# Deferring the last plain column block's eviction into the first Strassen-like unit of each FFN, with its gate product on VectorE

## Chip, cores and metric

One core of one Trainium2 chip. The metric is the device time of one execution in microseconds (us), the median of several runs; lower is better.

## What is computed

Two transformer blocks on x (512 tokens, width 1024), in float32. Three gated feed-forward networks (FFN) stand in them: f0 closes the first block, f1 opens the second, f2 closes the second.

```
def swiglu(xn, w_gate, w_up, w_down):
    return (jax.nn.silu(xn @ w_gate) * (xn @ w_up)) @ w_down    # hidden width 2816 = 22 blocks of 128
```

Between and before them are attention, retention and gating mixers, which the change doesn't touch.

## The kernel before

**Numbers.** Every float32 operand of a product is split into a high part of reduced precision (ScalarE casts it) and a low part (the rest, by a subtraction on VectorE or GpSimd). A product is three matmuls: high by high, high by low, low by high.

**An FFN** (function `ffn`, L1324) runs over the 22 hidden column blocks in two halves of 11. Blocks 0 to 4 of the first half are *plain* (`NPLAIN = 5`): gate and up projections of 128 columns by 512 tokens, each 24 matmuls into one PSUM bank. Blocks 5 to 10 and the whole second half are *units* (function `unit`, L1239): gate and up of a block are computed together as a 2 by 2 block product with seven quarter products of 12 matmuls (128x256) in place of eight. In the order of issue they are B11, T1, T2, B21, B22, T3 and T4; T4 of a unit is issued in the middle of the next one. After each half come the down products.

**A plain block's eviction** (L1363 to L1370): VectorE multiplies the gate bank by the norm factors (`fg`, L1365), ScalarE takes tanh of half of it (`ft`, L1366), VectorE does the same multiplication for the up bank (`u`, L1367), GpSimd multiplies `u` by `fg` (L1368), VectorE forms `ft = (ft + 1) * u` (L1369), and `put_hidden` (L1316) writes the high part `hh` on ScalarE (L365) and the low part `hl` on VectorE (L372). `hh` and `hl` are read by the down products, much later. For block 4, `prepare_b` (L1220) stands ahead of the eviction: it splits the eight normed inputs into `xh` (ScalarE, L363) and `xl` (VectorE, L370), which the units read.

**A unit** (L1250 to L1294) puts B11 into bank `r1` and ScalarE copies it out (`fu`, L1251); T1 goes into the right half of bank `r23` and ScalarE copies it out (`ff`, L1256); T2 is added to `r1`, which is copied out (`fu`, L1267); B21 goes into the left half of `r23`, B22 onto its right half; VectorE then forms the gate (`fg`, L1279); T3 is added to `r1`, read by L1285. Between these the unit prepares the next unit's weights: ScalarE casts the raw weights `wh<-raw` (parts AB), then `wh<-s13f` (parts S13), later `wh<-s24f` (parts S24); the low parts of AB are two GpSimd subtractions, those of S13 and S24 one VectorE subtraction each (all L303). `parts_d` casts `whd` on ScalarE, with the low part `wld` on GpSimd, for this unit's own T4. The raw buffers so freed release the next loads on SyncE's queue (L194). There are four raw buffers and five buffers of parts.

After T1 a unit calls `self.flush()`, which runs what an earlier step left in `self.pending` (the T4 of the unit before), and runs what that returns (that unit's `put_hidden`) after T2's copy:

```
self.quarter(r23[:, 256:512], u.S13, 0, "T1", True)
nc.scalar.copy(f, r23[:, 256:512])
...
late = self.flush()
...
self.quarter(r1, u.S24, 0, "T2", False)
nc.scalar.copy(e[:, 256:512], r1)
if late is not None:
    late()
u.parts_d()
```

At the first unit of an FFN nothing is pending. What sets the order of work: engines run their queues in order. A compile-time scheduler orders instructions of no further constraint by their place in the program and their readiness by its own estimate; from the first unit of a run of units to the last, `in_order` (L1307) fixes each engine's instructions in the order in which they were traced. Block 4's eviction is traced ahead of that region. The PSUM dependence goes by bank: a matmul that writes one half of `r23` waits for a copy that reads the other half.

The place in question occurs three times per execution, once in each FFN: the step from plain block 4 to unit 5, below called an *entry*.

Of the kernel before, what the change touches and what calls it, by code (L numbers as in the profile page):

```python
# [13 lines left out]
ALU = mybir.AluOpType  # L14
# [16 lines left out]
NPLAIN = 5  # L31
# [302 lines left out]
class Build:  # L334
# [145 lines left out]
    def plan(self):  # L480
# [63 lines left out]
        for m in range(KD):  # L544
            feat(f"o{m}", "w_out", m * P)
        ffn("f0", "w_ffn_down")
        ffn("f1", "ffn1_w_down_2")
        tok("t20", "w_in_2", KD, 1408, 1536, (1664, 1840))
        for key, c in (("kc", 1024), ("vc", 1152), ("ks", 1280), ("kw", 1536)):
# [16 lines left out]
        for m in range(KD):  # L566
            feat(f"o2{m}", "w_out_2", m * P)
        ffn("f2", "ffn2_w_down_2", True)
        return out

# [753 lines left out]
    def ffn(self, tag, scale, gain, hooks, on_out, begun=None, each=None, last=None):  # L1324
        nc, att = self.nc, self.att
        n = 0
        self.th, self.tl, self.ynorm = [], [], {}
        for half in range(2):
            hh, hl = [], []
            for i in range(11):  # L1330
                if half or i >= NPLAIN:
                    if i in (0, NPLAIN):
                        start = len(self.traced())
                    self.unit(f"{tag}{half}{i}", hh, hl, i)
                    if i == 10:
                        self.in_order(start)
                        self.last_step = [x for x in self.traced() if x.engine == mybir.EngineType.DVE][-1]
                    continue
                acc = []
                for w in "gu":  # L1340
                    wh, wl = self.ws.next(f"{tag}{w}{half}{i}")
                    self.ws.run_ahead()
                    if i == 1:

                        if w == "g":
                            early = self.ps.tile([P, 1024], F32, tag="ss", name=self.nm("early"), bufs=2)
                        b = early[:, 512 * (w == "u"):512 * (w == "u") + 512]
                    else:
                        b = self.bank("mm")
                    self.drain(self.tgroup(b, [(wh[:, k, :], wl[:, k, :], self.xh[k], self.xl[k]) for k in range(KD)]))  # L1350
                    acc.append(b)
                    if n < len(hooks):
                        hooks[n]()
                    n += 1
                    if n == 2 * NPLAIN - 1:
                        u = self.first_unit(f"{tag}0{NPLAIN}")
                        u.hi24()
                        u.lo24()
                if i == 0 and begun is not None:
                    begun()  # L1360
                if i == NPLAIN - 1:
                    self.prepare_b()
                tl = lambda t, bufs=1: att.tile([P, 512], F32, tag=t, name=self.nm(t), bufs=bufs)  # L1363
                g, th, u = tl("fg"), tl("ft", 2), self.small.tile([P, 512], F32, tag="sq", name=self.nm("u"), bufs=1)
                nc.vector.tensor_tensor(out=g, in0=acc[0], in1=self.rb, op=ALU.mult)  # L1365
                nc.scalar.activation(th, g, AF.Tanh, scale=0.5)  # L1366
                nc.vector.tensor_tensor(out=u, in0=acc[1], in1=self.rb, op=ALU.mult)  # L1367
                nc.gpsimd.tensor_tensor(out=u, in0=u, in1=g, op=ALU.mult)  # L1368
                nc.vector.scalar_tensor_tensor(out=th, in0=th, scalar=1.0, in1=u, op0=ALU.add, op1=ALU.mult)  # L1369
                self.put_hidden(i, th, 0.5, hh, hl)  # L1370
                if i < 4:
                    self.prepare_t(i, gain)
            if half == 1 and last is not None:
                last(hh, hl)
                return
            for m in range(KD):
                b = self.bank("mm")
                for p, (k0, k1) in enumerate(((0, 6), (6, 11))):
                    wh, wl = self.ws.next(f"{tag}d{half}{m}")
                    self.ws.run_ahead()  # L1380
                    for k in range(k0, k1):
                        self.mm3(b, wh[:, k - k0, :], wl[:, k - k0, :], hh[k], hl[k], k == 0, k == 10)
                    if m == 0 and p == 0:
                        self.flush()()
                    if half == 0 and (m, p) == (KD - 2, 1):
                        u = self.first_unit(f"{tag}10")
                    if half == 0 and (m, p) == (KD - 1, 0):
                        u.hi24()
                        u.lo24()
                x = self.xs[m]  # L1390
                if half == 0 and each is not None:
                    with self.tc.issue_after(self.last_step):
                        each(half, m)
                if scale == 1.0:
                    nc.vector.tensor_tensor(out=x, in0=b, in1=x, op=ALU.add)
                else:
                    nc.vector.scalar_tensor_tensor(out=x, in0=b, scalar=scale, in1=x, op0=ALU.mult, op1=ALU.add)
                if half == 1:
                    on_out(m, x)
# [659 lines left out]
```

## Time and profile before

| what | value |
|---|---|
| median of 3 runs | 2061.87 us (2060.95 to 2062.26) |
| the profiled execution's own time | 2062.82 us |
| its span, first to last instruction | 2061.0 us |
| TensorE (PE) busy | 98% |
| VectorE (DVE) / ScalarE (ACT) / GpSimd (POOL) busy | 71% / 50% / 27% |
| mean granted TensorE clock | 0.996 of full speed |

Busy times are shares of the span. A PE matmul's end is modelled: consecutive matmuls overlap in the records, so starts are the better measure of its pace. The clock column is the share of full speed (2.4 GHz) that was granted; the lower level is 1.2 GHz, 0.5 of it.

### The profile page before, as it was taken

How to read it: one execution, taken by the hardware profiler on the slowest of the kernel's cores; microseconds unless marked ns; L12 is line 12 of the kernel's file. 1: busy time of each engine (PE TensorE's matmuls, PEld its weight loads, DVE VectorE, ACT ScalarE, POOL GpSimd, SP SyncE). 2: the span in 40 equal slices, each digit the busy share in tenths (PEclk: the TensorE clock that was granted, in tenths of full speed). 3: DMA queues.
4: the chain of work that ended last, by engine and by line, in shares of the span. 5: the costliest groups of instructions: out<-in, count | busy, mean ns of one | idle time of the engine just before them, and what ended most of it. 6: DMA issues, size and time to landing. Idle time of an engine off the chain costs nothing. (4 is left out here: it accounts for less than half of the span.)

```text
span 2061.0 us, 31305 instructions
## 1 busy us (share of the span) xinstructions
PE 2019.5 (98%) x11694; PEld 1746.3 (85%) x11694; DVE 1466.9 (71%) x2727; ACT 1040.6 (50%) x1944; POOL 550.1 (27%) x463
## 2 busy tenths in 40 slices
PE   9999999999999999999999999999999999999998
PEld 7787878889899889899987778888888888989997
DVE  7678776686487487668648799888557757756865
ACT  7666753354355435335435576666343333533554
POOL 1233233331132333124235211110312233312310
PEclk9999999999999999999999999999999999999999
DMA  6323254214234322333455313222543442232353
GB/s 202 77 69 96 90 162 132 90 60 117 92 103 122 114 72 90 105 99 102 129 160 157 96 54 86 77 67 72 171 131 103 125 146 72 85 111 94 106 176 127
DMA packets 229527, 223.60 MB, mean 108 GB/s; under 512 B 16784, under 2 KB 190992, under 8 KB 229376
## 3 DMA queue, kind: packets, MB, share of 16 engines
q1 hardware_dynamic: 222992, 203.94, 32.9%
q0 software_dynamic: 5024, 15.90, 2.4%
q10 hardware_dynamic: 1360, 1.77, 0.3%
q8 instruction: 92, 1.51, 0.3%
q14 instruction: 59, 0.48, 0.1%
HBM read 204.11 MB, written 14.68 MB: 106 GB/s over the span
## 5 line engine op out<-in xcount | busy, mean ns | idle before, releaser
L236 DVE TENSOR_TENSOR wl<-raw,wh 128x1024 fp32r<-128x1024 f32 (+5 forms) x267 | 321.4, 1206 | 164.8 <-ACT wh L235 163.7
L235 ACT CAST wh<-raw 128x1024 fp32r<-128x1024 f32 (+5 forms) x267 | 252.2, 948 | 359.5 <-PE mm L397 289.5
L396 PE MATMUL mm<-xh,wh 128*128 128x512 f32 x888 | 363.0, 409 | 1.8 <-ACT th L363 1.4
L397 PE MATMUL mm<-xl,wh 128*128 128x512 f32 x888 | 349.8, 394 | 1.9 <-DVE xl L370 1.9
L398 PE MATMUL mm<-xh,wl 128*128 128x512 f32 x888 | 350.2, 395 | 0.0
L303 POOL TENSOR_TENSOR wl<-raw,wh 128x512 fp32r<-128x512 f32 x102 | 133.4, 1329 | 267.1 <-PE mm L1195 152.0
L398 PEld LDWEIGHTS mm<-xh,wl 128*128 128x128 f32 x888 | 167.0, 188 | 35.5
L396 PEld LDWEIGHTS mm<-xh,wh 128*128 128x128 f32 x888 | 167.6, 189 | 29.8 <-ACT th L363 2.6
L397 PEld LDWEIGHTS mm<-xl,wh 128*128 128x128 f32 x888 | 167.8, 189 | 28.3 <-DVE xl L370 3.7
L397 PE MATMUL mm<-hl,wh 128*128 128x512 f32 x440 | 172.8, 393 | 0.8 <-DVE hl L372 0.8
L398 PE MATMUL mm<-hh,wl 128*128 128x512 f32 x440 | 172.9, 393 | 0.0
L396 PE MATMUL mm<-hh,wh 128*128 128x512 f32 x440 | 171.2, 389 | 0.0
L613 ACT ACTIVATE P<-s,st 128x128 f32<-128x128 f32 (+1 forms) x192 | 101.3, 529 | 58.3 <-DVE st L608 54.2
L303 POOL TENSOR_TENSOR wld<-raw,whd 128x512 fp32r<-128x512 f32 x51 | 69.5, 1362 | 217.6 <-ACT whd L300 130.3
L1195 PE MATMUL pt<-xh,wh 128*128 128x256 f32 x408 | 114.9, 282 | 7.2 <-ACT ff L1256 7.2
L1195 PE MATMUL pt<-xl,wh 128*128 128x256 f32 x408 | 114.8, 281 | 0.0
L1195 PE MATMUL pt<-xh,wl 128*128 128x256 f32 x408 | 114.8, 281 | 0.0
L1195 PE MATMUL mm<-th,wh 128*128 128x256 f32 x408 | 113.3, 278 | 0.0
L1195 PE MATMUL mm<-tl,wh 128*128 128x256 f32 x408 | 112.9, 277 | 0.0
L1195 PE MATMUL mm<-th,wl 128*128 128x256 f32 x408 | 112.8, 276 | 0.0
L363 ACT CAST ph<-pt 128x128 fp32r<-128x128 f32 x192 | 80.3, 424 | 55.0 <-PE pt L631 53.8
L451 POOL TENSOR_TENSOR sacc<-sacc,sq 128x512 f32<-128x512 f32 x36 | 57.2, 1589 | 165.5 <-ACT sq L449 162.8
(482 smaller groups left out, 5462.3 us busy)
## 6 DMA issues: line engine op xcount, KB each, us to landing
raw<-in_gu_f SPq DMA_DIRECT2D x132, 512.0 KB
raw<-in_w_in SPq DMA_DIRECT2D x79, 512.0 KB
raw<-in_ffn_w_down SPq DMA_DIRECT2D x22, 512.0 KB
raw<-in_ffn_w_down SPq DMA_DIRECT2D x24, 384.0 KB
sp_th<-gt SPq DMA_DIRECT2D x32, 256.0 KB
raw<-in_w_out SPq DMA_DIRECT2D x16, 512.0 KB
raw<-in_ffn_w_down SPq DMA_DIRECT2D x24, 320.0 KB
raw<-in_w_ffn_down SPq DMA_DIRECT2D x16, 384.0 KB
```

The costliest lines, as they stand in the source:

```text
L235: nc.scalar.copy(p[0][:, :nk * nc_], src)
L236: nc.vector.tensor_tensor(out=p[1][:, :nk * nc_], in0=src, in1=p[0][:, :nk * nc_].bitcast(F32), op=ALU.subtract)
L303: (eng or self.ws.b.nc.vector).tensor_tensor(out=p[1], in0=src, in1=p[0].bitcast(F32), op=ALU.subtract)
L363: self.nc.scalar.copy(out, in_)
L396: mm(acc, lhsT=lh, rhs=rh, start=start, stop=False)
L397: mm(acc, lhsT=lh, rhs=rl, start=False, stop=False)
L398: mm(acc, lhsT=ll, rhs=rh, start=False, stop=stop)
L451: (eng or nc.gpsimd).tensor_tensor(out=acc, in0=acc, in1=dst, op=ALU.add)
L613: nc.scalar.activation(p, b, AF.Exp, bias=st[:, 0:1], scale=-1.0, accum_out=st[:, 1:2])
L1195: self.nc.tensor.matmul(acc, lhsT=l[:, sl], rhs=r, start=start and k + n == 0, stop=k == 3 and n == 2, skip_group_check=True)
```

## The change

For block 4 alone, the last three steps of the eviction (the product of `u` and `fg`, the `ft` step, `put_hidden`) are no longer traced ahead of the first unit. They are put into `self.pending`, so that unit 5 runs the product and the `ft` step after T1 and its copy `ff`, and `put_hidden` after T2 and its copy `fu`. The product of block 4 goes from GpSimd to VectorE. Blocks 0 to 3 run as before.

```
--- before.py
+++ after.py
@@ -1365,9 +1365,16 @@
                 nc.vector.tensor_tensor(out=g, in0=acc[0], in1=self.rb, op=ALU.mult)
                 nc.scalar.activation(th, g, AF.Tanh, scale=0.5)
                 nc.vector.tensor_tensor(out=u, in0=acc[1], in1=self.rb, op=ALU.mult)
-                nc.gpsimd.tensor_tensor(out=u, in0=u, in1=g, op=ALU.mult)
-                nc.vector.scalar_tensor_tensor(out=th, in0=th, scalar=1.0, in1=u, op0=ALU.add, op1=ALU.mult)
-                self.put_hidden(i, th, 0.5, hh, hl)
+
+                def close(i=i, g=g, th=th, u=u):
+                    (nc.vector if i == NPLAIN - 1 else nc.gpsimd).tensor_tensor(out=u, in0=u, in1=g, op=ALU.mult)
+                    nc.vector.scalar_tensor_tensor(out=th, in0=th, scalar=1.0, in1=u, op0=ALU.add, op1=ALU.mult)
+                    return lambda: self.put_hidden(i, th, 0.5, hh, hl)
+
+                if i == NPLAIN - 1:
+                    self.pending = close
+                else:
+                    close()()
                 if i < 4:
                     self.prepare_t(i, gain)
             if half == 1 and last is not None:
```

## Rows read from the trace of the kernel before

**Rows 1.** The page: busy time of each engine, its share and instructions.

```profile
PE 2019.5 (98%) x11694; PEld 1746.3 (85%) x11694; DVE 1466.9 (71%) x2727; ACT 1040.6 (50%) x1944; POOL 550.1 (27%) x463
```

**Rows 2.** Waits of PE, by line waited for: us in total, times, longest.

```profile
PE pt L1195 <- ACT ff L1256: 7.2, 3, 2.4
PE mm L396 <- DVE feat L852: 3.4, 2, 2.7
PE s L1618 <- DVE blkhl L370: 2.4, 1, 2.4
```

**Rows 3.** Timeline of PE, third entry: start us, us, ..., [idle before <- releaser].

```profile
1763.32 0.28 PE L1195 MATMUL pt<-th,wl 128*128 128x256 f32 x1
...
1764.88 0.28 PE L1195 MATMUL mm<-th,wl 128*128 128x256 f32 x1
...
1767.57 0.44 PE L1195 MATMUL pt<-xh,wh 128*128 128x256 f32 x1 [2.40 <-ACT ff L1256]
```

**Rows 4.** Timeline of ACT, third entry.

```profile
1766.62 0.63 ACT L365 ACTIVATE hh<-ft 128x512 fp32r<-128x512 f32 x1 [3.20 <-DVE ft L1369]
1767.16 0.35 ACT L1256 COPY ff<-pt 128x256 f32<-128x256 f32 x1
1767.41 1.05 ACT L300 CAST wh<-raw 128x1024 fp32r<-128x1024 f32 x1
...
1769.27 0.38 ACT L1267 COPY fu<-mm 128x256 f32<-128x256 f32 x1
1769.53 0.64 ACT L300 CAST whd<-raw 128x512 fp32r<-128x512 f32 x1
1770.25 1.01 ACT L300 CAST wh<-s24f 128x1024 fp32r<-128x1024 f32 x1
```

**Rows 5.** Timeline of DVE, third entry.

```profile
1763.44 0.68 DVE L1367 TENSOR_TENSOR u<-mm,rb 128x512 f32<-128x512 f32 x1
1764.05 0.68 DVE L370 TENSOR_TENSOR xl<-y,xh 128x512 fp32r<-128x512 f32 x1
1765.90 0.69 DVE L1369 SCALAR_TENSOR_TENSOR ft<-ft,u 128x512 f32<-128x512 f32 x1 [1.17 <-POOL u L1368]
...
1769.41 1.23 DVE L303 TENSOR_TENSOR wl<-s13f,wh 128x1024 fp32r<-128x1024 f32 x1 [1.43 <-ACT wh L300]
...
1775.42 0.69 DVE L284 TENSOR_TENSOR s13f<-raw 128x512 f32<-128x512 f32 x1
```

**Rows 6.** Timeline of POOL, third entry.

```profile
1764.27 1.59 POOL L1368 TENSOR_TENSOR u<-u,fg 128x512 f32<-128x512 f32 x1 [8.15 <-DVE u L1367]
1768.54 2.54 POOL L303 TENSOR_TENSOR wl<-raw,wh 128x512 fp32r<-128x512 f32 x2 [2.67 <-ACT wh L300]
1771.03 1.29 POOL L303 TENSOR_TENSOR wld<-raw,whd 128x512 fp32r<-128x512 f32 x1
```

**Rows 7.** The stretch behind each entry's PE wait: clock after the POOL column.

```profile
438.70:445.00 6.30, 6.30 (x40) 6.30 (x41) 3.37 (x5) 4.13 (x6) 3.76 (x3) 0.73 0.24 73
786.87:793.00 6.13, 6.13 (x39) 6.13 (x40) 3.18 (x4) 4.14 (x6) 3.78 (x3) 0.72 0.23 65
1767.57:1774.00 6.43, 6.43 (x41) 6.43 (x42) 3.34 (x4) 4.24 (x6) 3.78 (x3) 0.73 0.25 82
```

**Rows 8.** Chain of waits, third entry, steady unit: start us, us, what.

```profile
1776.43 2.79 PE mm L1195 x24
```

**Rows 9.** Stretches around two other PE waits: L852 (first), L1618 (second).

```profile
154.50:206.00 51.50, 48.05 (x243) 39.15 (x242) 44.20 (x101) 35.06 (x80) 17.83 (x20) 0.97 0.36 96
1081.50:1133.00 51.50, 46.70 (x229) 37.74 (x228) 44.70 (x55) 27.02 (x42) 26.64 (x18) 1.00 0.55 157
```

**Rows 10.** Timeline of POOL and DVE at an earlier plain block of f2.

```profile
1730.33 2.56 POOL L1368 TENSOR_TENSOR u<-u,fg 128x512 f32<-128x512 f32 x1 [0.67 <-DVE u L1367]
...
1730.50 1.22 DVE L236 TENSOR_TENSOR wl<-raw,wh 128x1024 fp32r<-128x1024 f32 x1
```

**Rows 11.** Timeline of SyncE's queue, third entry.

```profile
1771.10 1.57 SPq L194 DMA_DIRECT2D raw<-in_gu_f  x2
```

## The prediction

> **What bounds the kernel now.** I read the page first: PE is busy for 98% of the span [rows 1], so only time in which PE stands still, or runs slowly, can be won. The waits of PE come next. Their largest entry is the one the change aims at: 7.2 us in three waits of 2.4 us each, all for ACT's copy `ff` [rows 2], one at each entry. The timelines of the third entry show why. T1's last matmul starts at 1763.32 and is over 0.28 us later, at 1763.60; T2's last starts at 1764.88; the next, B21's first, only at 1767.57 [rows 3]. It writes the bank that `ff` reads, and `ff` runs at 1767.16, though its input was there at 1763.6. In ACT's queue it stood behind `hh`, which started at 1766.62 after 3.20 us of idleness [rows 4]. `hh` waited for DVE's `ft` (1765.90), and that for POOL's product (1764.27, 1.59 us) [rows 5, 6]. So PE waits for an eviction that nobody needs yet.
>
> A second cost follows each wait. In the 6.1 to 6.4 us behind it the mean granted clock is 0.73, 0.72 and 0.73 [rows 7]: part of each stretch ran at 1.2 GHz instead of 2.4. Before the waits PE was working without a break.
>
> **Step 1: `hh` leaves its place ahead of `ff`.** At the third entry `ff` can start at 1763.6 and, with its 0.35 us [rows 4], ends at about 1763.95. PE then wants B21 at 1765.0: T2's last start, plus one matmul's spacing of 2.79 / 24 = 0.116 us [rows 8]. The bank is free 1 us before that, so the wait goes as a whole. Measured from start to start it is 1767.57 - 1764.88 - 0.12 = 2.57 us per entry (the 2.4 of the waits view counts from a modelled end). Three entries: **7.7 us**. The waits view says that the three are alike.
>
> **Step 2: the clock behind the wait.** The three stretches lose 6.30 x 0.27 = 1.70, 6.13 x 0.28 = 1.72 and 6.43 x 0.27 = 1.74 us [rows 7], together **5.2 us**. Is this bound to the wait? All three entries show it. Elsewhere it is less sure: the stretch that holds the L852 wait of 2.7 us has 0.97, the one that holds the L1618 wait of 2.4 us has 1.00 [rows 2, 9]. A wait of such a length may or may not bring the clock down, but the low stretches at the entries begin behind one. With no wait I take the whole 5.2; the bounds are 0 (the clock falls all the same) and 5.2.
>
> **Step 3: what the moved step costs at its new place.** Four instructions move per entry: the product and `ft` (DVE), `hh` (ACT), `hl` (DVE). None issues a DMA. I lay out the third entry anew.
>
> - ACT: `ff` to 1763.95; AB cast 1.05 to 1765.0; S13 cast, as large as S24's 1.01, to 1766.0; the copy `fu` 0.38 to 1766.4; then `hh` 0.63 to 1767.0; `whd` 0.64 to 1767.7; S24's cast 1.01 to 1768.7 [rows 4].
> - DVE: `u` and the last `xl` end at 1764.73, as now. The product on DVE has no row. Its nearest one is that `xl` subtraction, of the same size and type with two SBUF inputs: 0.68 us [rows 5], which I take. The bounds are nothing and POOL's own 2.56 [rows 10]. It ends at 1765.4, `ft` (0.69) at 1766.1, in time for `hh`. Behind them stand S13's subtraction (1.23 [rows 5]) to 1767.3 and `hl`, as long as `ft`, to 1768.0.
> - PE: quarters of 12 x 0.116 = 1.39 us [rows 8]: B21 to 1766.4, B22 to 1767.8, T3 to 1769.2, the next unit's B11 to 1770.6 and T1 to 1771.9, then T4 and T2 (at 1773.3).
>
> The added wait is ACT's, for `ft` ahead of `hh`; behind it queue `whd`, S24's cast and the tanh. `whd` with its POOL part is wanted by T4 at 1771.9, S24 by T2 at 1773.3. POOL starts AB's two subtractions at 1765.0 and ends them at 1767.5 (2.54), `wld` (1.29) at 1768.9 [rows 6], three us early. S24's subtraction on DVE, as long as S13's, is done at about 1770, three us early. The gate of B22 can start at 1768.0 instead of 1767.8; its 0.2 us reach PE only through a bank that it takes again a unit later. So I cost the step at nothing on PE; its cover is the three us of lead. If the product took the full 2.56 instead of 0.68, `hh` and all behind it would be 1.6 us later and still in time: `ft` would end at 1768.0 and `hh` start there, not at 1766.4.
>
> SyncE's queue is passed by nothing, but its loads shift with POOL. Now AB's subtractions end at 1771.08, a raw load issues at 1771.10 [rows 6, 11], and DVE's first sum of the unit after runs at 1775.42 [rows 5], 4.3 us later. Then it would be 1767.5 and about 1771.2 (2 us behind T3's end, as now), 3.7 us. If the load needs all of the 4.3, DVE waits 0.6 us; its sums are for a T1 nearly a unit off. Nothing on PE.
>
> **Step 4: the product's engine.** DVE gains 3 x 0.68 = 2 us of work, POOL loses 3 x 1.59. With `hh` out of the way neither is on PE's path: on POOL the product would end at 1765.86 as now, `ft` at 1766.6, and `hh` would start 0.2 us later than in my layout. I give this part 0 by itself. The new `fg` of unit 5 uses the buffer that the product reads; both are DVE's now, in order, so no wait comes from that.
>
> There is one thing against the new place. POOL's AB subtractions now run beside three DVE instructions with two SBUF inputs each: the product's end, `ft` and `hl`. A POOL product took 2.56 us while DVE ran a 1.22 us subtraction with two SBUF inputs, against 1.27 for half of the pair of 2.54 [rows 6, 10]: about the DVE instruction's length on top. Here that adds 0.4 + 0.69 + 0.69 = 1.8 us at most, so AB ends at 1769.3 where B11 wants its first half at 1769.2, and that half is the first of the two to be written. I take 0. At the bound of 2.56 for each of the two, AB ends at 1770.1; if B11 waited for both, that is 0.9 us per entry, 2.8 in all. The Trainium skill (GPSIMD Engine Reference, Key points) says that GpSimd shares its SBUF interfaces with VectorE and contends with VectorE instructions of two SBUF inputs. That speaks against moving this product to VectorE at a time when GpSimd is working; by that rule the sum would lose those 2.8 us, by the layout nothing.
>
> **The sum.** 7.7 + 5.2 = 12.9 us of the profiled execution's 2062.82. That execution stands 0.95 us over the median of 2061.87; the same 12.9 off the median gives **2049.0 us**. All later work is started by PE's results or by freed buffers, so it moves up with PE; nothing in the trace is tied to absolute time.
>
> **The rivals.**
>
> - *The wait goes and the clock falls all the same.* For it: a wait is not always followed by a low clock [rows 9], so something else at the entry (the change to 256-wide matmuls) may share in it. Against: it stands behind the wait in all three. Only 7.7 come back: 2061.87 - 7.7 = 2054.2. Chance 0.08.
> - *It doesn't do what it says:* `hh` still gets ahead of `ff`, as the scheduler placed it before. Against: `hh` is now traced behind `fu`, inside the region of fixed order. Only the product's engine then counts: `ft` would start at 1765.4 instead of 1765.9, 3 x 0.5 = 1.5 us: 2060.4. Chance 0.06.
> - *Slower:* AB's low parts come late. DVE's two-input instructions hold POOL off, and the next unit's B11 stands where B21 stood, again with a low clock behind. It begins to cost when POOL ends AB after 1769.2, and turns the sign once that is 2.57 + 1.7 = 4.3 us later, at 1773.5, 8.5 us after the cast instead of 2.5. If the pair took 10 us, each entry would lose 1.5: 2061.87 + 4.5 = 2066.4. For it: the 2.56 of one row [rows 10]; against: twice that is only 5.1. Chance 0.04.
>
> **How the numbers follow.** My forecast has 0.82, of which the reach is 2047 to 2052: down, the 0.95 us between profile and median and a low stretch elsewhere that may vanish with shifted times; up, the 2.8 of the port, or one low clock more (1.7) at a wait like L1618's. The range takes in the first rival with 0.4 us of scatter: 2047.0 to 2054.6; it leaves out the other two and a few of the forecast's own cases. A measurement of this kernel can tell about 0.2%, 4.1 us, from no change. Faster by more than that are the forecast and the first rival, 0.90; the second is within it, 0.06; the third slower, 0.04.
>
> **What would show it.** Right: no wait of PE on `ff` at the entries; `ff` some 0.4 us behind T1's last start, `hh` behind the copy `fu` of L1267; clock near 1.00 in the first unit; B21's first matmul one spacing after T2's last; a span of about 2048. Step 2 is wrong if the first unit still shows a clock of about 0.73 without a wait; step 3 if PE waits at T3, T4, T2 or the next B11, for `fu`, `wld`, S24 or AB's low parts; step 4 if AB's two POOL subtractions take more than 4 us.

## The result and the profile after

The changed kernel takes 2050.9 us in the median (2049.84 to 2051.97, 6 runs), the kernel before 2062.31 beside it (2060.95 to 2063.79, 6 runs): 11.4 us less, ratio 0.9942 with a 95% interval of 0.9933 to 0.9952. The profiled execution took 2051.97 us, with a span of 2050.2 (before: 2062.82 and 2061.0). Run five times more in the second group of experiments it gave 2051.47, ratio 0.9943 (0.9931 to 0.9955).

The waits of PE come first, as before. The three largest are:

```profile
PE mm L396 <- DVE feat L852: 3.4, 2, 2.7
PE s L1625 <- DVE blkhl L370: 2.4, 1, 2.4
PE mm L396 <- ACT gt L956: 2.1, 1, 2.1
```

The entry of 7.2 us for `ff`, which led the list of before [rows 2], is gone. No wait of a PE matmul on L1195, the line of all quarter products, is left in the list. The timeline of PE at the third entry (T2's last two matmuls, then B21's first, and T4's first in the unit after) shows the seam closed:

```profile
1757.78 0.28 PE L1195 MATMUL mm<-tl,wh 128*128 128x256 f32 x1
1757.90 0.28 PE L1195 MATMUL mm<-th,wl 128*128 128x256 f32 x1
1758.02 0.28 PE L1195 MATMUL pt<-xh,wh 128*128 128x256 f32 x1
...
1765.08 0.28 PE L1195 MATMUL mm<-th,whd 128*128 128x256 f32 x1
```

B21 starts 0.12 us after T2's last matmul; before it was 2.69 [rows 3]. ACT's timeline there gives the reason:

```profile
1756.79 0.37 ACT L1256 COPY ff<-pt 128x256 f32<-128x256 f32 x1 [0.34 <-PE pt L1195]
1757.06 1.06 ACT L300 CAST wh<-raw 128x1024 fp32r<-128x1024 f32 x1
1758.01 1.02 ACT L300 CAST wh<-s13f 128x1024 fp32r<-128x1024 f32 x1
1758.91 0.39 ACT L1267 COPY fu<-mm 128x256 f32<-128x256 f32 x1
1760.10 0.63 ACT L365 ACTIVATE hh<-ft 128x512 fp32r<-128x512 f32 x1 [0.80 <-DVE ft L1371]
```

`ff` now waits for PE's T1 and for nothing else; `hh` stands four places later and still idles 0.80 us for `ft`, where no PE work hangs on it at once. DVE and POOL in the same stretch:

```profile
1757.67 0.68 DVE L1370 TENSOR_TENSOR u<-u,fg 128x512 f32<-128x512 f32 x1
1758.38 1.68 DVE L1371 SCALAR_TENSOR_TENSOR ft<-ft,u 128x512 f32<-128x512 f32 x1
...
1763.45 0.41 DVE L1285 TENSOR_TENSOR fw<-mm,ff 128x256 f32<-128x256 f32 x1
```

```profile
1758.19 3.04 POOL L303 TENSOR_TENSOR wl<-raw,wh 128x512 fp32r<-128x512 f32 x2 [9.05 <-ACT wh L300]
```

The product takes 0.68 us on DVE, against 1.59 on POOL [rows 6]. The `ft` step, which meets POOL's pair, takes 1.68 instead of 0.69 [rows 5], and the pair 3.04 instead of 2.54 [rows 6]. The clock in the stretches that answer to [rows 7] and [rows 9] (it stands behind the POOL column):

```profile
435.62:442.00 6.38, 6.38 (x57) 6.38 (x56) 6.34 (x8) 4.20 (x7) 4.80 (x3) 1.00 0.31 87
779.53:786.00 6.47, 6.47 (x57) 6.47 (x56) 6.40 (x9) 4.19 (x7) 4.82 (x3) 1.00 0.27 85
1758.02:1764.40 6.38, 6.38 (x57) 6.38 (x56) 6.34 (x8) 4.34 (x8) 4.68 (x3) 1.00 0.30 87
...
154.50:206.00 51.50, 47.23 (x247) 38.37 (x245) 45.10 (x103) 34.84 (x80) 17.92 (x20) 1.00 0.35 92
1081.50:1133.00 51.50, 45.68 (x213) 36.29 (x211) 38.61 (x50) 24.65 (x39) 29.72 (x19) 0.97 0.53 149
```

All three entries run at full clock; before they had 0.72 to 0.73. The two other places have changed sides: the stretch of the L852 wait had 0.97 and has 1.00, that of the wait at L1625 (L1618 before) had 1.00 and has 0.97.

### The profile page after: what moved, and what is told of

It reads as the page before. It is cut to its first block, busy times and chain, and to the rows that moved or that the text cites. A ratio compares the mean times of both kernels' runs of the same rounds, so it can differ in the third digit from the quotient of the medians.

```text
span 2050.2 us, 31305 instructions
## 1 busy us (share of the span) xinstructions
PE 2016.3 (98%) x11694; PEld 1743.6 (85%) x11694; DVE 1467.2 (72%) x2730; ACT 1040.4 (51%) x1944; POOL 549.4 (27%) x460
## 5 line engine op out<-in xcount | busy, mean ns | idle before, releaser
L397 PE MATMUL mm<-xl,wh 128*128 128x512 f32 x888 | 350.0, 395 | 1.9 <-DVE xl L370 1.9
L397 PEld LDWEIGHTS mm<-xl,wh 128*128 128x128 f32 x888 | 167.8, 189 | 28.1 <-DVE xl L370 3.7
L397 PE MATMUL mm<-hl,wh 128*128 128x512 f32 x440 | 172.6, 392 | 0.8 <-DVE hl L372 0.8
L1195 PE MATMUL mm<-th,wh 128*128 128x256 f32 x408 | 113.0, 277 | 0.0
L1195 PE MATMUL mm<-th,wl 128*128 128x256 f32 x408 | 112.8, 276 | 0.0
L1195 PE MATMUL pt<-xl,wh 128*128 128x256 f32 x408 | 112.8, 276 | 0.0
L1195 PE MATMUL pt<-xh,wl 128*128 128x256 f32 x408 | 112.8, 276 | 0.0
L1195 PE MATMUL mm<-tl,wh 128*128 128x256 f32 x408 | 112.8, 276 | 0.0
L1195 PE MATMUL pt<-xh,wh 128*128 128x256 f32 x408 | 112.8, 276 | 0.0
```

The costliest lines, as they stand in the source:

```text
L397: mm(acc, lhsT=lh, rhs=rl, start=False, stop=False)
L1195: self.nc.tensor.matmul(acc, lhsT=l[:, sl], rhs=r, start=start and k + n == 0, stop=k == 3 and n == 2, skip_group_check=True)
```

## The experiments

Eight kernels in two groups of four, with five runs each (eleven for two of them), beside the kernel before, whose median was 2062.99 in the first group and 2062.84 in the second (15 runs each). Times are medians. Lines of an edit with - and + go by the changed kernel, unless said otherwise.

**Only the deferral, product on GpSimd.**

```
-                    (nc.vector if i == NPLAIN - 1 else nc.gpsimd).tensor_tensor(out=u, in0=u, in1=g, op=ALU.mult)
+                    nc.gpsimd.tensor_tensor(out=u, in0=u, in1=g, op=ALU.mult)
```

> The changed kernel with block 4's product back on GpSimd; only the deferral is left. Theory (the deferral carries the gain, the engine of the product is off PE's path): PE doesn't wait for ff at the entries, hh starts some 0.2 to 0.5 us later than in the changed kernel, and the time is that of the changed kernel, 2050.9 us, within 2. Rival (the product's engine carries a share): 2 us or more slower than the changed kernel, with a wait of PE on ff, wld or S24 at the entries.

Measured: 2055.48 us, ratio 0.9963 (0.9951 to 0.9976), 4.6 more than the changed kernel's 2050.9 (4.3 by the two ratios). PE doesn't wait for `ff`. Another wait is there. PE's waits, then the third entry on POOL, on DVE and on PE:

```profile
PE mm L1195 <- DVE fw L1285: 3.8, 3, 1.3
```

```profile
1760.19 2.56 POOL L303 TENSOR_TENSOR wl<-raw,wh 128x512 fp32r<-128x512 f32 x2 [8.90 <-ACT wh L300]
1762.69 1.30 POOL L1370 TENSOR_TENSOR u<-u,fg 128x512 f32<-128x512 f32 x1
```

```profile
1764.03 0.69 DVE L1371 SCALAR_TENSOR_TENSOR ft<-ft,u 128x512 f32<-128x512 f32 x1 [4.14 <-POOL u L1370]
1764.64 1.22 DVE L303 TENSOR_TENSOR wl<-s13f,wh 128x1024 fp32r<-128x1024 f32 x1
1765.77 0.68 DVE L372 SCALAR_TENSOR_TENSOR hl<-ft,hh 128x512 fp32r<-128x512 f32 x1
1766.37 0.69 DVE L1279 TENSOR_TENSOR fg<-pt,fu 128x512 f32<-128x512 f32 x1
1766.97 1.22 DVE L303 TENSOR_TENSOR wl<-s24f,wh 128x1024 fp32r<-128x1024 f32 x1
1768.10 0.42 DVE L1285 TENSOR_TENSOR fw<-mm,ff 128x256 f32<-128x256 f32 x1
```

```profile
1768.66 0.36 PE L1195 MATMUL mm<-th,whd 128*128 128x256 f32 x1 [1.27 <-DVE fw L1285]
```

Read it backwards. T4 adds to the bank that `fw` must read first. `fw` is the sixth of an unbroken row of DVE instructions that begins with `ft`; `ft` had DVE idle for 4.14 us; and its product, though its inputs were there, ran on POOL only after AB's pair, since in the region of fixed order it is traced behind that pair. Theory's "the engine of the product is off PE's path" falls: 1.3 us at each of three entries.

**Only the engine, nothing deferred.** The edit is against the kernel before.

```
-                nc.gpsimd.tensor_tensor(out=u, in0=u, in1=g, op=ALU.mult)
+                (nc.vector if i == NPLAIN - 1 else nc.gpsimd).tensor_tensor(out=u, in0=u, in1=g, op=ALU.mult)
```

> The kernel before with nothing changed but the product of block 4 on VectorE; the eviction still stands ahead of the first unit. Theory: hh still runs ahead of ff and PE waits for ff three times, each about 0.5 us shorter (1.9 instead of 2.4), with the low clock behind still there: 2060.8 us, 1.5 less than before. Rival (the product's engine carries the gain): 2055 or less.

Measured: 2055.03 us, ratio 0.9962 (0.9949 to 0.9974): 8.0 less than before, where theory said 1.5. ACT's timeline at the third entry:

```profile
1758.37 0.37 ACT L1256 COPY ff<-pt 128x256 f32<-128x256 f32 x1 [0.20 <-PE pt L1195]
1758.63 1.05 ACT L300 CAST wh<-raw 128x1024 fp32r<-128x1024 f32 x1
1761.80 0.63 ACT L365 ACTIVATE hh<-ft 128x512 fp32r<-128x512 f32 x1 [2.12 <-DVE ft L1369]
1762.34 0.99 ACT L300 CAST wh<-s13f 128x1024 fp32r<-128x1024 f32 x1
1763.23 0.38 ACT L1267 COPY fu<-mm 128x256 f32<-128x256 f32 x1
```

`hh` is no longer ahead of `ff`, but behind the AB cast. Nothing in the source says so: with the product on DVE the compile-time scheduler came to another order on ACT, at all three entries. The wait for `ff` is gone. `hh` now holds up S13's cast and the copy `fu`, and PE waits there in its place:

```profile
PE mm L1195 <- ACT fu L1267: 2.8, 3, 0.9
```

So one edit of a VectorE line moved a ScalarE instruction, and that brought its 8 us: from the start of T2's last matmul to that of the last in the next unit's T1 each entry returned 3.0 us, where the changed kernel's return 4.2.

**Only `put_hidden` deferred.** The edit is against the kernel before.

```
                 nc.gpsimd.tensor_tensor(out=u, in0=u, in1=g, op=ALU.mult)
                 nc.vector.scalar_tensor_tensor(out=th, in0=th, scalar=1.0, in1=u, op0=ALU.add, op1=ALU.mult)
-                self.put_hidden(i, th, 0.5, hh, hl)
+                put = lambda i=i, th=th: self.put_hidden(i, th, 0.5, hh, hl)
+                if i == NPLAIN - 1:
+                    self.pending = lambda: put
+                else:
+                    put()
```

> The kernel before with only put_hidden of block 4 (hh and hl) deferred to the place behind T2's copy; product on GpSimd and the ft step stay ahead of the first unit. Theory (hh's place in ScalarE's queue is the whole cause): the same as the changed kernel, 2050.9 us within 2, no wait of PE on ff. Rival (VectorE's order or the ft step counts too): at least 3 us slower than the changed kernel.

Measured: 2051.67 us, ratio 0.9943 (0.9930 to 0.9955), the changed kernel's ratio to 0.0001. PE's list has no wait on L1195. The product is on GpSimd, as in the first experiment, but runs ahead of AB's pair:

```profile
1755.02 1.63 POOL L1369 TENSOR_TENSOR u<-u,fg 128x512 f32<-128x512 f32 x1 [8.15 <-DVE u L1367]
1756.60 3.01 POOL L303 TENSOR_TENSOR wl<-raw,wh 128x512 fp32r<-128x512 f32 x2
```

This settles two things. The place of `put_hidden` is worth the whole change, within the scatter of the two ratios; `hl` on DVE moves with `hh` and wasn't tested apart, but PE's wait was for `ff`, which stood behind `hh` on ACT. And POOL's speed didn't cost the 4.6 us of the first experiment: at 1.63 us the product is as slow as before, and nothing is lost when it stands ahead of AB's pair.

**A wait put back without the old order.** Seven ScalarE copies into a buffer that isn't in use yet, ahead of `ff`, in the first unit of each FFN.

```
+        if key[2:] == f"0{NPLAIN}":
+            for _ in range(7):
+                nc.scalar.copy(th, self.xs[0])
         nc.scalar.copy(f, r23[:, 256:512])
```

> The changed kernel with seven ScalarE copies (128x512) into the unit's not yet used ft tile ahead of ff, in the first unit of each FFN only: a wait of PE on ff of about the old size, 2.5 us, comes back without the old eviction order. Theory (the low clock follows the wait): three waits of 2 to 3 us, a granted clock of about 0.73 in the 6 us behind each, and 11 to 14 us over the changed kernel: 2062 to 2065. Rival (the low clock belongs to something else at the entry): the waits alone, 6 to 9 us: 2057 to 2060, clock near 1.00 behind them.

Measured: 2065.68 us (2064.19 to 2066.71, 11 runs), 14.8 over the changed kernel, with three waits of 3.0 us:

```profile
PE pt L1195 <- ACT ff L1259: 9.0, 3, 3.0
```

The stretches behind them (clock behind the POOL column):

```profile
439.05:445.40 6.35, 6.35 (x53) 6.35 (x54) 4.50 (x6) 5.00 (x8) 4.27 (x3) 1.00 0.25 74
786.00:792.20 6.20, 6.20 (x40) 6.20 (x41) 3.82 (x4) 4.67 (x7) 4.23 (x3) 0.74 0.21 69
1769.61:1776.00 6.39, 6.39 (x31) 6.39 (x32) 3.06 (x4) 4.11 (x7) 4.21 (x3) 0.52 0.25 72
```

The waits bring the low clock back although the eviction's order is the new one: the time is more than the 9.0 us of the waits, which the rival allowed. But not each time: the first of the three is followed by 1.00. The timed runs agree: the mean granted clock of the 11 is 0.9949, against 0.9975 for the changed kernel's 11, which by the estimate explained under step 2 below is 5.3 us more lost; with the 9.0 of the waits that makes 14.3 of the 14.8. In the first experiment, whose waits were 1.3 us, the stretches behind all three had 1.00.

**The changed kernel again, and with four more VectorE products ahead of `ft`.**

> The changed kernel once more, as it is, beside the kernels of this group. Both theories expect 2051 us within 1.5 and no wait of PE on ff. In its profile the low clock may or may not stand behind the waits of L852 (2.7 us) and L1625 (2.4 us), which have nothing to do with the entries: if it changes from one profile to the next with the same program, it is decided by the execution, and not by the change.

Measured: 2051.47 us, no wait on L1195. The wait of L852 was 2.7 us again, with 1.00 behind it as in the first profile. That of L1625 was 0.8 instead of 2.4 us: in this profile the low clock came already behind a wait of 1.4 us at L397 (0.73 from 1084.30 to 1090.70), and PE reached L1625 later. So the same program can have its low clock at another place in another execution.

```
                     (nc.vector if i == NPLAIN - 1 else nc.gpsimd).tensor_tensor(out=u, in0=u, in1=g, op=ALU.mult)
+                    if i == NPLAIN - 1:
+                        for _ in range(4):
+                            nc.vector.tensor_tensor(out=g, in0=u, in1=u, op=ALU.mult)
```

> The changed kernel with four more VectorE products of 128x512 (into the fg buffer, which nobody reads any more) behind block 4's product at each entry: 4 x 0.6 = 2.4 us of VectorE work ahead of the ft step. Theory (the nearest lead is T4's, which waits until VectorE's fw has read the bank, 1.2 us after fw's end in the changed kernel): PE waits at each T4 for fw for 0.5 to 1.3 us, 1.5 to 4 us slower than the changed kernel: 2052.5 to 2055. Rival (the lead is the three us of the prediction's layout): no wait of PE at the entries, 2051 within 1.5.

Measured: 2061.28 us (2056.77 to 2063.38, 11 runs), 9.8 over the changed kernel. Both ideas were too kind. The waits, the stretches from each T1 wait on (clock behind the POOL column), the four products, and POOL's pair:

```profile
PE mm L1195 <- DVE fw L1285: 3.9, 3, 1.3
...
PE pt L1195 <- DVE wl L303: 2.8, 3, 0.9
```

```profile
442.55:451.00 8.45, 7.14 (x59) 6.96 (x60) 8.28 (x12) 4.82 (x9) 4.67 (x3) 1.00 0.18 62
788.95:797.00 8.05, 6.74 (x42) 6.57 (x43) 7.89 (x12) 4.42 (x8) 4.65 (x3) 0.79 0.21 67
1771.10:1779.00 7.90, 6.59 (x55) 6.42 (x56) 7.73 (x12) 4.26 (x7) 4.66 (x3) 1.00 0.20 66
```

```profile
1764.48 4.83 DVE L1373 TENSOR_TENSOR fg<-u 128x512 f32<-128x512 f32 x4
```

```profile
1764.15 3.15 POOL L303 TENSOR_TENSOR wl<-raw,wh 128x512 fp32r<-128x512 f32 x2 [8.91 <-ACT wh L300]
```

T4 waits for `fw`, as theory said. But the four products took 4.83 us and not 2.4: the two that met POOL's pair took 1.67 each, the two behind it 0.69. So DVE was later than meant, and the next unit's T1 waits too, for S13's subtraction behind `ft` on DVE. At the second entry the low clock stands behind these waits (0.79). From T2's last matmul to the next unit's B22 the three entries together return 9.6 us less than in the changed kernel, nearly the whole difference. The lead that the prediction's layout saw, three us, isn't there; the changed kernel has no room for four more such instructions.

**Two attempts at the waits that are left.** First the split of a compressed block in the second mixer, traced ahead of the next block's sums:

```
+            if kind == "k":
+                hlk = kp.tile([P, 16, P], F32R, tag="blkhl", name=self.nm("blkhl"))
+                self.hi(hlk[:, :, 0:64], blk[kind])
+                self.lo(hlk[:, :, 64:128], blk[kind], hlk[:, :, 0:64])
         for kind in "kv":
...
```

(Further down, block k takes this `hlk` instead of making its own.)

> The changed kernel, and in the second mixer the split of the first compressed block (ScalarE's cast and VectorE's subtraction, blkhl) is traced ahead of the second block's four sums. PE's wait at L1625 of 2.4 us should fall by the two or four sums that stood ahead (0.7 us each), to 1.0 or less, and with it the chance of a low clock behind: 1.4 to 4 us faster than the changed kernel, 2047 to 2049.5. Rival (something else is late next there): no change, 2051.

Measured: 2050.11 us, ratio 0.9940 (0.9928 to 0.9953), no difference to the changed kernel that can be measured. The wait is 2.4 us as before, `PE s L1632 <- DVE blkhl L370`: two of the four sums went behind the subtraction, but PE came to it earlier by as much. The order of PE's queue explains it: 6419 matmuls stand ahead of the first that waits, where 6425 did, and those six, 0.23 us apart there, are the two sums' 1.4. The edit doesn't ask for that; it is an order that changed with it, like that of `hh` above.

Then, on top of it, the rotation of q behind four feature products:

```
...
-            self.rope_q(qr)
             w = self.ws.next("kv")
             self.ws.run_ahead()
             yield from feats(1, w, ch[2:], cl[2:], rbkv)
+            self.rope_q(qr)
```

> As v1_blk_split, and in the first mixer the rotation of q (rope_q, L1003 on VectorE and GpSimd) is traced behind the next four feature products in place of ahead of them. PE's waits at L852 (2.7 and 0.7 us) should go, with the low clock that follows in some executions: 2 to 4 us faster than v1_blk_split. Rival (the rotation is then late for the attention scores that read it): the wait comes back there, no change or slower.

Measured: 2049.14 us, ratio 0.9932 (0.9919 to 0.9946). The L852 wait is gone from the list, and a wait at L692 of 2.8 us for POOL's `krs` heads it. It is the lowest median of all, 2.3 us under the changed kernel in its group, but the two intervals overlap, so it isn't shown to be faster.

## Why the prediction was right

**Step 1** (the wait goes: 7.7 us) came out as written. All three waits are gone, and nothing at the entries took their place. Compare the same matmul in both traces: T2's last at the third entry started 6.98 us earlier than before (1757.90 for 1764.88), T1's last in the next unit 11.18 us earlier (1764.97 for 1776.15), so that entry returned 4.2 us, as did each of the other two. The layout's 2.57 + 1.74, for steps 1 and 2 together, is 4.3.

**Step 2** (the low clock goes with it: 5.2 us) was right too. Putting a wait back brought the low clock back, so the link is shown. That the low clock belongs to something else at the entry, the first rival, is ruled out: in the seven profiles of the changed kernel (two), the first three experiments and the last two kernels, none with a wait for `ff`, the clock is 1.00 in the first unit at all 21 entries. The experiment with four more products has waits of its own there.

The forecast of 12.9 us in all is 1.5 more than the 11.4 measured, but these runs can't tell the two apart: the interval of the ratio stands for 9.9 to 13.8 us. At the entries the profile returned 3 x 4.2 = 12.6. Its span fell by 10.8 only, so 1.8 us went elsewhere; where was not followed. In the second profile of the changed kernel the span is 14.7 below that of before. So the rest of an execution scatters by more than the forecast is off. The clock of the timed runs fits, less exactly: the 30 of before in the two groups have a mean granted clock of 0.9956, the changed kernel's 11 runs 0.9975 (each run's is given to 0.001). Time lost, estimated as one minus that, times the time, is 9.1 us before and 5.2 after; the 3.9 that came back are uncertain by 1.9 (95%, from the scatter of the runs), so the step's 5.2 isn't excluded. In the profile of after, the gain at L852 and the loss at L1625 cancel, 51.5 x 0.03 = 1.5 us each, as far as a share of two digits tells. The prediction had named such a loss as part of the upward side of its range.

**Step 3** (the moved step costs PE nothing) held for the kernel as it is, but its cover was read wrongly. Against the layout's "three us early" stands T4's first matmul at 1765.08 and the end of `fw` at 1763.86: 1.2 us. The step asked who waits for `whd`, `wld` and S24, and forgot that T4 also waits for a reader of its bank, `fw`, and that DVE would run from the product to `fw` without a gap. By the layout's own times `fw`, behind S24's subtraction that ends at about 1770, had some 1.5 us, so its sentence that a product of 2.56 us would still be in time was wrong as well. The experiment with four more products found that end, and the first one found it at three entries.

**Step 4** gave the product's engine 0. This is the step that failed, and that the total was right in spite of it is luck. Given the deferral, DVE is worth 4.6 us. The step let POOL run the product "as now", at once; but deferral also puts it behind AB's pair in POOL's queue, and I moved the step past ACT's queue and DVE's, not past POOL's. It happened to be covered because the change does both.

The bound on POOL's side of the port was sound: the pair took 3.04 us, less than the 5.1 of the bound, and PE didn't notice. But the layout put the whole price on POOL, and most of it fell on DVE: `ft` took 1.68 us instead of 0.69. The Trainium skill (GPSIMD Engine Reference, Key points), by which GpSimd contends with VectorE instructions of two SBUF inputs, agrees with those rows; the last section has one such meeting that cost nothing. Here it cost 1.0 us on DVE and 0.5 on POOL, and none on PE, since DVE's `fw` was still 1.2 us early.

**The second rival** (hh stays ahead of `ff`, only the engine counts: 2060.4) was not what happened. Its price stays untested, since no run has the product on DVE with `hh` ahead of `ff`: the engine alone gave 8 us, because the scheduler's order isn't fixed ahead of the region and changed with the product's engine. **The third** (slower, by a starved POOL) did not come near: 3.04 us for the pair against the 8.5 that would have turned the sign.

## What to carry to other kernels

When a wait is at a copy, look in that engine's queue for what stands ahead of it and isn't needed yet; moving it (`hh` here, with its `hl`) behind the copy was worth all of it. The product and the `ft` step need not have moved: once they were deferred too, the change of engine was what kept that from costing 4.6 us. A deferred instruction lands at a new place in every queue it uses: list for each what is ahead of it there, and for each buffer that a later matmul writes who must read it first. And where a compile-time scheduler orders the queues, compare the orders of both programs before pricing an edit, since an edit on one engine can move instructions on another.

## What the runs showed of the hardware

A low clock doesn't follow every like wait of PE. At the L852 wait of 2.7 us, up to which nine of the ten profiled programs (all but the last) run the same instructions, the stretch from 154.50 to 206.00 has 0.97 or 0.93 in six profiles and 1.00 in three, the changed kernel's two among these. At the entries a low clock stood behind all three waits of 2.4 us, behind two of three of 3.0 us, behind none of three of 1.3 us, and behind one of three of 1.3 us that came 1.4 us after a wait of 0.9 us. The changed kernel's five runs of the second group go from 2048.08 to 2053.02 us, with mean clocks from 0.995 to 0.998.

A VectorE product or `ft` step of two SBUF inputs, 0.68 us alone, took 1.67 or 1.68 us when it began beside AB's first or second GpSimd subtraction of the same size; each ended 0.55 us behind that subtraction (1760.06 after 1759.51 in the changed kernel). The pair of GpSimd subtractions took 3.04 and 3.15 us in these meetings instead of 2.54. Not every meeting costs that: in the kernel before, S13's subtraction on VectorE, also of two SBUF inputs, took 1.23 us beside a pair of 2.54 [rows 5, 6].
